# Reloading x for its scaling, and when the weight additions and gate stores of twelve tile pairs are issued, in a hybrid decoder step

## The chip, the cores and the metric

The kernel runs on one core of a Trainium2 chip. The metric is device time in microseconds for one execution of the whole step, lower being better. TensorE (PE) does the matmuls, VectorE (DVE), ScalarE (ACT) and GpSimd (POOL) work on tiles in on-chip memory, and SyncE (SP) issues most transfers. A transfer is issued from an engine's instruction queue, in that queue's order; if it must wait for something, what stands behind it in the queue waits too.

## The reference

One layer: an RMSNorm, one wide input projection that is split into column groups, two branches (sparse attention and an mLSTM recurrence) for a prompt of 1024 tokens and eight decode requests, and one output projection.

```python
h = x * rsqrt(mean(x * x) + eps) * norm_w                # x: 1024 prompt rows + 8 sample rows, 2048 wide
aq, ak, av, iq, ik, iw, az, mq, mk, mv, mi, mf, mo, mz = split(h @ w_in)
att   = sparse_attend(aq, ak, av, top_k(indexer(iq, ik, iw)))        # prompt
att_s = the same for 8 requests, keys and values gathered from a paged cache
h_ml  = mlstm(mq, mk, mv, mi, mf)                        # in chunks of 64, carrying C, n, m
a     = att * silu(az)
mo    = rmsnorm(h_ml) * ml_norm_w * sigmoid(mo) * silu(mz)
y     = final_rmsnorm(x + concat(a, mo) @ w_out)
```

## The kernel before

**Data.** x lies transposed on chip: 16 row groups of 128 model rows, each with R = 1032 columns (1024 prompt tokens and 8 samples). Every f32 operand of a product is split into a high and a low part, and a product is three matmuls (high by high, low by high, high by low). The first 256 columns of x are in tiles named xP, the next 776 in xQ, of which the first four row groups have the last 388 in xR; psum tiles are `pj` and `bank`.

**Tiles.** The input projection runs over 61 tiles of 128 output columns, in the order of `T_MISC` (0), index queries (1 to 8), attention keys `T_AK` (9), values (11), queries (13), mLSTM queries, keys and values (21, 25, 29), gates `T_G` (37 to 52, for each head the output gate and the SiLU gate) and `T_AZ` (53 to 60). A tile is four quarters of four row groups. `proj()` loads a weight quarter (`wraw`, L219), splits it on ACT (L222, wH) and DVE (L223, wL), and multiplies (L1368).

**Start.** Tiles 0 to 2 run on x before it is scaled, since the reciprocal norm `rstd` is not known yet. During tiles 3 to 8 `rescale(k)` turns row group k into x times `rstd` (`norm_w` having been multiplied in at loading): DVE adds high and low (L1456) and multiplies (L1457), ACT makes the new high part (L1458), DVE the low one (L1459), and for k of 8 and up SyncE stores the row to `xS` (L1461). `sums(k)` makes sums and differences of scaled rows k and k + 4 (L1466 to L1469, `y` being 128 x 1032) and stores them to `sS` (L1470, L1471). Which of them follows which quarter stands in `plan` and `slots`. Tiles 4, 5 and 6 multiply unscaled quarters first and scaled ones last.

**Pairs.** From `T_S` (37) on, the tiles go in 12 pairs, in two phases of half of the row groups each: 24 pair-products v, worked in the manner of Strassen with fewer products (P0, P1, A11, A12, A22, S1 to S4) on sums of weights and of x. That is what `sS` is for. In a pair-product (L1591 for its matmuls):
- `wfetch()` loads weights; for two of the sums of weights (T1 in `wraw`, T3 in a slot named xP) SyncE loads one quarter (L1567, L1570) and GpSimd at once issues a second transfer that adds the other to it (L1568, L1571);
- `split()` makes high and low parts (L1576 on ACT, L1577 on DVE);
- `seed()` copies one psum tile to another, on ACT (L1671), for the product that goes on from it;
- `out()` takes results from psum (L1604, L1606, L1608). In phase 1 they are stored to `part`; in phase 2 GpSimd adds `part` to them by an accumulating transfer (L1613, xR<-part; the tiles are eight, in a ring), and the result's `use()` is put on the list `later`;
- `flush(2)` takes uses off that list until two are left. A use of a gate tile is a sigmoid on ACT (L1650, L1653), a product on DVE for the second tile of a pair (L1651), the product of both on GpSimd (L1656) and a store to `gateS` from SyncE (L1657). A use of a `T_AZ` tile multiplies by broadcast row factors (`rb`, loaded into an `ev` buffer; L1662 and L1664 on DVE), takes the sigmoid (L1665), the product on GpSimd (L1666) and stores (L1667).

**Side work.** Attention, index and mLSTM work is cut into pieces, in two lanes, each with jobs that follow one another. `Lane.step()` issues pieces after each quarter (or each `side(now)` of a pair-product) so that a job of a given weight ends at its due tile, the second number of `Job`. A job starts when its start tile is reached, the job before it in its lane is done, and its condition holds: prompt attention `att` waits for decode attention `datt`, `ml` follows `att`.

**Order.** Within these program sections a scheduler puts the instructions of each engine in order at build time, with the sections under `tc.high_priority()` or `hi()` first. After that, each engine executes in order.

## Time and profile before

| | |
|---|---|
| time, median of 2 runs | 2207.28 us (2202.98 to 2211.59) |
| the profiled execution's own time | 2206.24 us |
| its span in the trace | 2204.5 us |
| mean granted TensorE clock | 0.962 |
| busy in the span: PE / DVE / ACT / POOL | 93% / 56% / 46% / 16% |
| bytes moved | 319.58 MB, mean 145 GB/s |

An engine's busy share is an average over the whole span; the page also cuts the span in 40 slices of 55 us, one digit each in tenths. A stretch in which TensorE shows less than 9 is one in which something else ends last, and the lists of waits for that stretch say what: engine and line that waited, the instruction it waited for, then microseconds in total, the number of waits and the longest. A group of instructions is shown as line, engine, operation, tiles, count, busy us, mean ns, and the idle time ahead of them with what ended it.

### The profile page before, as it was taken

How to read it: one execution, taken by the hardware profiler on the slowest of the kernel's cores; microseconds unless marked ns; L12 is line 12 of the kernel's file. 1: busy time of each engine (PE TensorE's matmuls, PEld its weight loads, DVE VectorE, ACT ScalarE, POOL GpSimd, SP SyncE). 2: the span in 40 equal slices, each digit the busy share in tenths (PEclk: the TensorE clock that was granted, in tenths of full speed). 3: DMA queues.
4: the chain of work that ended last, by engine and by line, in shares of the span. 5: the costliest groups of instructions: out<-in, count | busy, mean ns of one | idle time of the engine just before them, and what ended most of it. 6: DMA issues, size and time to landing. Idle time of an engine off the chain costs nothing. (4 is left out here: it accounts for less than half of the span.)

```text
span 2204.5 us, 34897 instructions
## 1 busy us (share of the span) xinstructions
PE 2039.9 (93%) x12390; PEld 1945.4 (88%) x12390; DVE 1242.7 (56%) x2936; ACT 1017.7 (46%) x2114; POOL 342.6 (16%) x390
## 2 busy tenths in 40 slices
PE   9897999999999999869999999887797787999998
PEld 8896999999999999769999999887787777998886
DVE  8794354365554547835666655865665465656331
ACT  8232247733336773124555555654555243433221
POOL 0220111100000000410000001233334451111110
PEclk9998999999999999969999999999899898999999
DMA  6455543322222223626464446877687788648212
GB/s 229 116 179 166 164 130 96 107 85 71 74 68 63 63 65 77 195 78 184 128 164 136 123 106 194 241 202 185 165 230 146 154 246 293 187 152 293 86 62 97
DMA packets 239995, 319.58 MB, mean 145 GB/s; under 512 B 39397, under 2 KB 151973, under 8 KB 239821
## 3 DMA queue, kind: packets, MB, share of 16 engines
q1 hardware_dynamic: 217293, 278.01, 40.6%
q0 software_dynamic: 21376, 37.86, 9.5%
q8 instruction: 97, 1.59, 0.3%
q10 hardware_dynamic: 1152, 1.49, 0.2%
q14 instruction: 77, 0.63, 0.1%
HBM read 238.41 MB, written 78.86 MB: 144 GB/s over the span
## 5 line engine op out<-in xcount | busy, mean ns | idle before, releaser
L1368 PE MATMUL pj<-xQ,wH 128*128 128x388 f32 (+1 forms) x1832 | 484.1, 342 | 20.6 <-ACT xQ L1458 14.8
L1591 PE MATMUL pj<-xQ,wH 128*128 128x388 f32 x1344 | 374.6, 359 | 65.0 <-ACT pj L1671 52.3
L222 ACT CAST wH<-wraw 128x512 fp32r<-128x512 f32 (+2 forms) x279 | 169.6, 611 | 430.3 <-PE pj L1368 194.7
L1368 PEld LDWEIGHTS pj<-xQ,wH 128*128 128x128 f32 (+1 forms) x1832 | 328.9, 189 | 26.1 <-ACT xQ L1458 16.0
L223 DVE TENSOR_TENSOR wL<-wraw,wH 128x512 fp32r<-128x512 f32 (+2 forms) x279 | 193.5, 700 | 237.2 <-ACT wH L222 230.4
L1591 PEld LDWEIGHTS pj<-xQ,wH 128*128 128x128 f32 x1344 | 256.4, 200 | 71.1 <-ACT pj L1671 56.3
L1368 PE MATMUL pj<-xQ,wL 128*128 128x388 f32 (+1 forms) x916 | 312.6, 342 | 0.5 <-DVE wL L223 0.5
L1591 PE MATMUL pj<-xQ,wL 128*128 128x388 f32 x672 | 238.3, 355 | 1.2 <-DVE wL L1577 1.2
L1368 PE MATMUL pj<-xP,wH 128*128 128x256 f32 (+1 forms) x896 | 175.5, 286 | 1.3 <-ACT wH L222 1.1
L1368 PEld LDWEIGHTS pj<-xQ,wL 128*128 128x128 f32 (+1 forms) x916 | 172.9, 189 | 1.6 <-DVE wL L223 0.7
L1577 DVE TENSOR_TENSOR wL<-xP,wH 128x512 fp32r<-128x512 f32 x168 | 118.4, 708 | 61.8 <-ACT wH L1576 57.5
L1591 PE MATMUL pj<-xP,wH 128*128 128x256 f32 x768 | 146.1, 284 | 3.4 <-ACT xP L1543 3.4
L1368 PEld LDWEIGHTS pj<-xP,wH 128*128 128x128 f32 (+1 forms) x896 | 145.1, 188 | 3.9 <-ACT wH L222 1.7
L1576 ACT CAST wH<-xP 128x512 fp32r<-128x512 f32 x168 | 103.0, 615 | 75.1 <-PE pj L1591 63.4
L1591 PEld LDWEIGHTS pj<-xQ,wL 128*128 128x128 f32 x672 | 133.6, 199 | 2.2 <-DVE wL L1577 2.1
L1368 PE MATMUL pj<-xP,wL 128*128 128x256 f32 (+1 forms) x448 | 126.4, 282 | 3.6 <-DVE wL L223 3.6
L1591 PEld LDWEIGHTS pj<-xP,wH 128*128 128x128 f32 x768 | 122.6, 191 | 4.3 <-ACT xP L1543 3.6
L462 ACT ACTIVATE rl<-bank 128x512 f32<-128x512 f32 (+2 forms) x160 | 79.1, 522 | 78.9 <-PE bank L460 53.6
L465 DVE SCALAR_TENSOR_TENSOR s<-rl,wiN,s 128x512 f32<-128x512 f32 (+2 forms) x150 | 94.7, 656 | 35.5 <-ACT rl L462 33.0
L1591 PE MATMUL pj<-xP,wL 128*128 128x256 f32 x384 | 109.0, 284 | 0.9 <-DVE wL L1577 0.9
L1863 PE MATMUL bank<-mH,wH 128*128 128x392 f32 x256 | 89.3, 349 | 16.6 <-ACT wH L222 14.6
L505 ACT ACTIVATE gt<-s,sm 128x384 bf16<-128x384 f32 (+5 forms) x96 | 84.6, 881 | 24.1 <-DVE sm L527 17.7
(457 smaller groups left out, 4372.0 us busy)
## 6 DMA issues: line engine op xcount, KB each, us to landing
wraw<-in_wa_dram SPq DMA_DIRECT2D x166, 256.0 KB
xP<-in_wa_dram SPq DMA_DIRECT2D x120, 256.0 KB
wraw<-in_wo_dram SPq DMA_DIRECT2D x64, 256.0 KB
wraw<-in_wt_dram SPq DMA_DIRECT2D x64, 256.0 KB
part<-ev SPq DMA_DIRECT2D x48, 194.0 KB
xR<-part POOLq DMA_DIRECT2D x48, 194.0 KB
qkv<-mlS SPq DMA_DIRECT2D x16, 512.0 KB
xr<-in_xT_dram SPq DMA_DIRECT2D x14, 516.0 KB
```

What stands on the lines that cost most here:

```text
L222: a = SC.copy(H[:, s, :cols], raw[:, s, :cols])
L223: return a, V.tensor_tensor(L[:, s, :cols], raw[:, s, :cols], H[:, s, :cols].bitcast(F32), OP.subtract)
L462: SC.activation(r[:, :cn], p[:, :cn], AF.Relu)
L465: v = V.scalar_tensor_tensor(s[:, c0:c0 + cn], r[:, :cn], wv, s[:, c0:c0 + cn], OP.mult, OP.add)
L505: SC.activation(junk[:, :W], src[q][:, :W], AF.Sign, bias=bias[:, q:q + 1], scale=scale, accum_out=cnt[:, q:q + 1])
L1368: m = PE.matmul(ps[:cols, :cn], w_[:, k, :cols], xv(kk, xz, c0, cn), start=(n0 == 0 and k == 0 and z == 0), stop=(n0 == n9 and k == 3 and ...
L1576: SC.copy(H, src)
L1577: V.tensor_tensor(L, src, H.bitcast(F32), OP.subtract)
L1591: PE.matmul(ps[:, :n], w_[:, k, :], REG[reg][k](xz), start=(first and k == 0 and z == 0), stop=(last and k == 3 and z == 2), skip_group_ch ...
L1863: PE.matmul(p, w_[:, k, :], x_, start=(n == 0), stop=(n == 47))
```

## The change

Five things are edited.

1. **Scaling.** `xfetch()` loads the rows of x anew, the first five in advance and then one for each row that is scaled. `rescale(k)` multiplies such a row by `norm_w` and `rstd` in one DVE instruction over all 1032 columns (L1459), makes high (L1462) and low parts (L1463) from it, and stores all 16 rows to `xS` (L1464). There is one in each of 16 slots; `sums` is gone from there.
2. **Sums of x.** `xsums()` makes them in tiles 10 to 17: four loads from `xS` into `ev` buffers, the four DVE instructions, four stores to `sS`.
3. **Weight additions.** `wfetch()` only notes them in `adds`; `addup()` issues them (L1587), once after the first part's result and once before the third's.
4. **Gate uses.** The gates' product is on DVE (L1672) in place of GpSimd; the stores to `gateS` are issued by GpSimd (L1673, L1683) in place of SyncE; `flush(3)` leaves three uses on the list.
5. **Due times** of two jobs: prompt attention 47 for 46, decode attention 35.5 for 34.

```diff
@@ -1316,11 +1316,11 @@
 
     lanes = [Lane([Job("gates", T_AK, T_AK + 1.5, 8500, job_gates),
                    Job("index", T_AK, 30.0, 3000 + sum(map(ix_weight, groups)), lambda: job_index(groups)),
-                   Job("att", T_MQ, 46.0, 2 * 2 * sum(2 * (1 + (i + 1) * 0.5) for i in range(8)) + 6, job_att, att_free),
+                   Job("att", T_MQ, 47.0, 2 * 2 * sum(2 * (1 + (i + 1) * 0.5) for i in range(8)) + 6, job_att, att_free),
                    Job("ml", T_G, T_PRE, 38, job_ml)]),
              Lane([Job("dscore", T_AK, 18, 16 + 128 + 2, job_dscore),
                    Job("dsel", T_AK, 30.0, 2000 + 31 * 1700 + 10000 + 16 * 2800 + 2000, job_dsel),
-                   Job("datt", T_MQ, 34.0, 7500 + 8 * 5000 + 4000 + 8 * 2500 + 3000, job_datt, ix_free),
+                   Job("datt", T_MQ, 35.5, 7500 + 8 * 5000 + 4000 + 8 * 2500 + 3000, job_datt, ix_free),
                    Job("dml", T_G, T_PRE - 0.5, 20000 + 16 * 2500 + 5000, job_dml, dml_free)])]
     gateV = gateS.rearrange("(k p) r -> k p r", p=128)
     mixb = [[None] * KT for _ in CB]
@@ -1449,38 +1449,31 @@
                 evac(t, pss[t], 128, iqp)
         ys = {}
 
+        def xfetch(n):
+            for k in range(len(ys), min(KT, n)):
+                y = ys[k] = rp.tile([128, R], F32, name="y")
+                pin(SY.dma_start(y, A["xT"][k]))
+
         def rescale(k):
-            y = ys[k] = rp.tile([128, R], F32, name="y")
+            y = ys[k]
+            V.scalar_tensor_tensor(y, y, nw[:, k:k + 1], rstd, OP.mult, OP.mult)
             for c0, cn in CH if k < 4 else (CH[0], (PN, R - PN)):
-                h, l, e = xv(k, 0, c0, cn), xv(k, 1, c0, cn), y[:, c0:c0 + cn]
-                V.tensor_tensor(e, h.bitcast(F32), l.bitcast(F32), OP.add)
-                V.tensor_tensor(e, e, rstd[:, c0:c0 + cn], OP.mult)
-                SC.copy(h, e)
-                V.tensor_tensor(l, e, h.bitcast(F32), OP.subtract)
-            if k >= K_KEPT:
-                SY.dma_start(xS[k], y)
-
-        def sums(k):
-            y1, y2 = ys[k], ys[k + 4]
-            a11, a21, a12, a22 = (y[:, PN + x * HN:PN + x * HN + HN] for y in (y1, y2) for x in range(2))
-            V.tensor_tensor(a22, a22, a21, OP.subtract)
-            V.tensor_tensor(a21, a11, a21, OP.subtract)
-            V.scalar_tensor_tensor(a11, a22, -1.0, a11, OP.mult, OP.subtract)
-            V.scalar_tensor_tensor(a12, a11, -1.0, a12, OP.mult, OP.subtract)
-            SY.dma_start(sS[k], y1[:, PN:R])
-            SY.dma_start(sS[k + 4], y2[:, PN:R])
-
-        r, z = rescale, sums
-        plan = [(r, 0), (r, 1), (r, 2), (r, 3), (r, 4), (z, 0), (r, 5), (z, 1), (r, 6), (z, 2), (r, 7), (z, 3),
-                (r, 8), (r, 9), (r, 10), (r, 11), (r, 12), (z, 8), (r, 13), (z, 9), (r, 14), (z, 10), (r, 15), (z, 11)]
-        slots = {(3, 0): 1, (3, 1): 1, (3, 2): 1, (3, 3): 1, (4, 0): 1, (4, 1): 1, (4, 2): 1, (4, 3): 1, (5, 0): 2,
-                 (5, 1): 2, (5, 2): 1, (5, 3): 1, (6, 0): 1, (6, 1): 2, (6, 2): 2, (6, 3): 2, (7, 0): 2, (7, 1): 1}
+                h = xv(k, 0, c0, cn)
+                SC.copy(h, y[:, c0:c0 + cn])
+                V.tensor_tensor(xv(k, 1, c0, cn), y[:, c0:c0 + cn], h.bitcast(F32), OP.subtract)
+            SY.dma_start(xS[k], y)
+            xfetch(k + 6)
+
+        plan = list(range(KT))
+        slots = {(3, 0): 1, (3, 1): 1, (3, 2): 1, (3, 3): 1, (4, 0): 1, (4, 1): 1, (4, 2): 1, (4, 3): 1, (5, 1): 1,
+                 (5, 2): 1, (5, 3): 1, (6, 0): 1, (6, 1): 1, (6, 2): 1, (6, 3): 1, (7, 0): 1}
 
         def after(t, n):
             with tc.high_priority():
                 for _ in range(slots.get((t, n), 0)):
-                    f, k = plan.pop(0)
-                    f(k)
+                    rescale(plan.pop(0))
+
+        xfetch(5)
 
 
         for t in range(3, T_AK):
@@ -1503,8 +1496,25 @@
                 evac(t, ps, 128, iqp)
             if t == 3:
                 index_weights(misc)
+    def xsums(t, q):
+        k = t - T_AK - 1
+        if q or not 0 <= k < 8:
+            return
+        k += k // 4 * 4
+        a11, a21, a12, a22 = (evp.tile([128, CN], F32, name="ev") for _ in range(4))
+        for x, (l, r) in enumerate(((a11, a21), (a12, a22))):
+            for y, e in enumerate((l, r)):
+                SY.dma_start(e, xS[k + 4 * x][:, PN + y * HN:PN + y * HN + HN])
+        V.tensor_tensor(a22, a22, a21, OP.subtract)
+        V.tensor_tensor(a21, a11, a21, OP.subtract)
+        V.scalar_tensor_tensor(a11, a22, -1.0, a11, OP.mult, OP.subtract)
+        V.scalar_tensor_tensor(a12, a11, -1.0, a12, OP.mult, OP.subtract)
+        for x, (l, r) in enumerate(((a11, a21), (a12, a22))):
+            for y, e in enumerate((l, r)):
+                SY.dma_start(sS[k + 4 * x][:, y * HN:y * HN + HN], e)
+
     for t in range(T_AK, T_S - 2):
-        pss = proj((t,))
+        pss = proj((t,), after=xsums)
         with tc.high_priority():
             evac(t, pss[0], 128)
 
@@ -1547,6 +1557,7 @@
     slot = [None] * 8
     t1s = {}
     later = []
+    adds = []
     B11, B21, T2, T1, B22, B12, T3, T4 = range(8)
     hi = tc.high_priority
 
@@ -1565,10 +1576,15 @@
         elif j == T1:
             t1s[v] = wst.tile([128, 4, 128], F32, name="wraw", bufs=2)
             SY.dma_start(t1s[v], a1)
-            G.dma_start(t1s[v], b1, accum_op=OP.add)
+            adds.append((t1s[v], b1))
         elif j == T3:
             SY.dma_start(slot[j], b1)
-            G.dma_start(slot[j], b2, accum_op=OP.add)
+            adds.append((slot[j], b2))
+
+    def addup():
+        while adds:
+            t_, w_ = adds.pop(0)
+            G.dma_start(t_, w_, accum_op=OP.add)
 
     def split(j, v):
         H, L = (wst.tile([128, 4, 128], F32R, name="w" + x, bufs=3) for x in "HL")
@@ -1653,8 +1669,8 @@
                 SC.activation(e[:, :cn], e[:, :cn], AF.Sigmoid)
             if (n, c) in keep:
                 o = keep.pop((n, c))
-                G.tensor_tensor(e[:, :cn], o[:, :cn], e[:, :cn], OP.mult)
-                SY.dma_start(gateS[(8 + gi) * 128:(9 + gi) * 128, c0:c0 + cn], e[:, :cn])
+                V.tensor_tensor(e[:, :cn], o[:, :cn], e[:, :cn], OP.mult)
+                G.dma_start(gateS[(8 + gi) * 128:(9 + gi) * 128, c0:c0 + cn], e[:, :cn])
             else:
                 keep[n, c] = e
         else:
@@ -1664,7 +1680,7 @@
                 V.tensor_copy(rb[:, cp:cn], e[:, cp:cn])
             SC.activation(e[:, :cn], e[:, :cn], AF.Sigmoid)
             G.tensor_tensor(e[:, :cn], e[:, :cn], rb[:, :cn], OP.mult)
-            SY.dma_start(gateS[j * 128:(j + 1) * 128, c0:c0 + cn], e[:, :cn])
+            G.dma_start(gateS[j * 128:(j + 1) * 128, c0:c0 + cn], e[:, :cn])
 
     def seed(dst, src):
         if "index" in lanes[0].done:
@@ -1715,8 +1731,10 @@
 
     pj = [psj.tile([128, 512], F32, name=f"pj{c}") for c in range(3)]
     now = T_S * 4
+    addup()
     wfetch(T1, 0)
     wfetch(T1, 1)
+    addup()
     with hi():
         w0 = split(B11, 0)
     product(w0, pj[0], "A11", True, True)
@@ -1748,13 +1766,14 @@
         product(w1, C_, "P1", False, True)
         product(w1, B_, "A12", False, True)
         with hi():
+            addup()
             out(v, 0, 0, C_)
             w1 = split(T1, v)
             if move:
                 f2 = fill_load("A12", nx)
                 fill(f1)
                 fill(f2)
-        flush(2)
+        flush(3)
         side(now)
         product(w2, A_, "S2", False, True)
         with hi():
@@ -1771,10 +1790,11 @@
             w1 = split(B12, v)
             if move:
                 f2 = fill_load("S1", nx)
-        flush(2)
+        flush(3)
         side(now + 1)
         product(w2, B_, "S4", False, True)
         with hi():
+            addup()
             out(v, 1, 1, B_, sv)
             if move:
                 fill(f1)
@@ -1792,7 +1812,7 @@
                 fill(f1)
                 f3 = fill_load("P1", nx)
             w0 = split(B11, v + 1) if v + 1 < len(seq) else None
-        flush(2)
+        flush(3)
         side(now + 2)
         product(w2, A_, "S3", False, True)
         with hi():
@@ -1815,7 +1835,7 @@
                 fill(f2)
         if t >= T_AZ + 3 or pair_tiles(n)[1] == T_G - 1:
             flush()
-        flush(2)
+        flush(3)
         side(now + 3)
         now += 4
     flush()
```

The scheduler's order shows the change at three places. First VectorE, while x is scaled in tiles 4 to 6, before (y is a row of x; L223 splits weights for the tiles; iqe is an evacuation):

```order
L1466 TENSOR_TENSOR y<-y 128x388
L740 SCALAR_TENSOR_TENSOR fx<-fx,t_2058 32x128
L357 TENSOR_TENSOR iqe<-pj_1273,rstd 128x388
L223 TENSOR_TENSOR wL<-wraw,wH 128x512
L1466 TENSOR_TENSOR y<-y 128x388
L1467 TENSOR_TENSOR y<-y 128x388
L742 SCALAR_TENSOR_TENSOR b<-fx 32x128
L1467 TENSOR_TENSOR y<-y 128x388
L1468 SCALAR_TENSOR_TENSOR y<-y 128x388
L749 COPY e_2135<-b 32x1
L223 TENSOR_TENSOR wL<-wraw,wH 128x512
```

and in the changed kernel:

```order
L223 TENSOR_TENSOR wL<-wraw,wH 128x512
L1459 SCALAR_TENSOR_TENSOR y<-y,nw,rstd 128x1032
L742 SCALAR_TENSOR_TENSOR b<-fx 32x128
L1463 TENSOR_TENSOR xP_174<-y,xP_174 128x256
L1463 TENSOR_TENSOR xQ_160<-y,xQ_160 128x776
L223 TENSOR_TENSOR wL<-wraw,wH 128x512
L1459 SCALAR_TENSOR_TENSOR y<-y,nw,rstd 128x1032
L749 COPY e_2055<-b 32x1
L1463 TENSOR_TENSOR xP_175<-y,xP_175 128x256
L1463 TENSOR_TENSOR xQ_161<-y,xQ_161 128x776
L1459 SCALAR_TENSOR_TENSOR y<-y,nw,rstd 128x1032
```

Between two weight splits stood sums of two rows; now the scalings of the next rows stand there, one instruction of 1032 columns and two subtractions each.

Second TensorE, in tiles 33 to 36, where decode attention ends (L1256 to L1289, whose last are matmuls of four columns on gathered values) and prompt attention begins (L574, L611). Before:

```order
L1256 MATMUL bank<-cst,lT 64x128
L1258 MATMUL bank<-onesf,kn 64x1
L1256 MATMUL bank<-cst,lT 64x128
L1276 MATMUL bank<-cst,P 128x64 x2
L1277 MATMUL bank<-cst,pb 128x64
L1289 MATMUL bank<-PT,kv 128x4 x32
L574 MATMUL bank<-cst,pP 128x128 x8
L611 MATMUL bank<-kH,qH 128x512
L611 MATMUL bank<-kL,qH 128x512
```

and now, from the same place on:

```order
L1276 MATMUL bank<-cst,P 128x64 x2
L1277 MATMUL bank<-cst,pb 128x64
L1289 MATMUL bank<-PT,kv 128x4 x12
L1368 MATMUL bank<-xP_175,wH 128x256 x2
L1368 MATMUL bank<-xP_175,wL 128x256
L1368 MATMUL bank<-xP_175,wH 128x256 x2
L1368 MATMUL bank<-xP_175,wL 128x256
L1368 MATMUL bank<-xP_175,wH 128x256 x2
L1368 MATMUL bank<-xP_175,wL 128x256
L1368 MATMUL bank<-xP_175,wH 128x256 x2
L1289 MATMUL bank<-PT,kv 128x4
L1368 MATMUL bank<-xP_175,wL 128x256
```

The L1289 matmuls were all together with L574 right behind them; now products of the projection (L1368) stand between them, and L574 comes some fifty rows later.

Third GpSimd in phase 2, in pair-products of the gate tiles (L841, L840, L872 to L874 are mLSTM side work). Before:

```order
L1613 DMA xR_10543<-part_9718 128x256
L1568 DMA wraw<-in_wa_dram 128x512
L1613 DMA xR_10544<-part_9718 128x388
L841 TENSOR_SCALAR aL<-onec 128x2x2
L1571 DMA xP_10104<-in_wa_dram 128x512
L1613 DMA xR_10544<-part_9718 128x388
L840 CAST aH<-onec 128x2x2
L1613 DMA xR_10545<-part_9718 128x256
L1656 TENSOR_TENSOR xR_10544<-xR_10544 128x388
L1613 DMA xR_10545<-part_9718 128x388
```

and now:

```order
L1629 DMA xR_10304<-part_9565 128x388
L1587 DMA xP_9844<-in_wa_dram 128x512
L1673 DMA gateS<-xR_10303 128x388
L1629 DMA xR_10301<-part_9565 128x256
L841 TENSOR_SCALAR aL<-onec 128x2x2
L840 CAST aH<-onec 128x2x2
L1629 DMA xR_10301<-part_9565 128x388
L1673 DMA gateS<-xR_10304 128x388
L872 TENSOR_SCALAR st<-st 128x2
L873 TENSOR_TENSOR st<-st,mhalf 128x2
L1673 DMA gateS<-xR_10301 128x256
```

The weight additions (L1568, L1571, now L1587) stood between accumulations of results; the products (L1656) are gone from this queue, and stores to `gateS` (L1673) have come, each behind some later accumulations.

## The prediction

> **What bounds the kernel now.** I read the page first, for the engine that the time belongs to, then the same engine in stretches of the span, and then only what it waits for in the stretches where it is short. Parts 1 and 2 of the page:
>
> ```profile
> PE 2039.9 (93%) x12390; PEld 1945.4 (88%) x12390; DVE 1242.7 (56%) x2936; ACT 1017.7 (46%) x2114; POOL 342.6 (16%) x390
> PE   9897999999999999869999999887797787999998
> PEclk9998999999999999969999999999899898999999
> ```
>
> TensorE is the bound, and most of its slices are full. It is short in four places: near the start, at the 19th and 20th slice, in the long run from the 26th on, and once near the end. Nothing outside them can bring time, because the change takes no matmul away. The table of windows gives their size (columns: window, length, PE busy and its matmuls, granted clock, DMA share, GB/s; two rows also have the busy times of PEld, DVE, ACT and POOL, in this order):
>
> ```profile
> 60.00:200.00 140.00, 116.36 (x615) 0.90 0.56 168
> 100.00:110.00 10.00, 10.00 (x58) 1.00 0.76 216
> 300.00:500.00 200.00, 200.00 (x1343) 198.91 (x1342) 97.46 (x258) 117.13 (x280) 23.32 (x28) 1.00 0.32 97
> 850.00:900.00 50.00, 50.00 (x352) 1.00 0.53 152
> 900.00:1000.00 100.00, 72.78 (x386) 0.78 0.39 115
> 1250.00:1300.00 50.00, 50.00 (x336) 1.00 0.34 93
> 1404.00:1773.00 369.00, 294.26 (x1739) 283.11 (x1739) 212.31 (x620) 184.83 (x392) 133.41 (x185) 0.91 0.76 186
> ```
>
> I turn counts into lost time. **A**, 60 to 200 us (tiles 3 to 8, x being scaled): a full 10 us holds 58 matmuls, so 615 need 106 us and 34 are lost. **B**, 900 to 1000 (tiles 33 to 35, decode attention ending and prompt attention beginning): at 352 in 50 us, 386 need 55 and 45 are lost, though some of them are tiny. **C**, 1404 to 1773, ten pair-products of the second phase: at 336 in 50 us, 1739 need 259 and 110 are lost, 11 in each of 36.9. **D** is the switch to the output projection near 1840.
>
> **A: scaling.** The waits of PE and DVE, then the groups of DVE, in 60 to 200 us:
>
> ```profile
> PE pj L1368 <- ACT xQ L1458: 14.8, 2, 9.4
> PE pj L1368 <- ACT xR L1458: 4.5, 1, 4.5
> DVE y L1456 <- DMA sS<-y: 9.4, 6, 4.1
> L1457 DVE TENSOR_TENSOR y<-y,rstd 128x256 f32<-128x256 f32 (+2 forms) x36 | 21.2, 626 | 0.0
> L1459 DVE TENSOR_TENSOR xQ<-y,xQ 128x776 fp32r<-128x776 f32 (+1 forms) x16 | 13.6, 856 | 4.5 <-ACT xQ L1458 4.5
> L1456 DVE TENSOR_TENSOR y<-xQ 128x776 f32<-128x776 f32 (+1 forms) x16 | 13.4, 857 | 0.0
> L1456 DVE TENSOR_TENSOR y<-xP 128x256 f32<-128x256 f32 x16 | 6.4, 420 | 9.5 <-DMA sS<-y 9.4
> L1466 DVE TENSOR_TENSOR y<-y 128x388 f32<-128x388 f32 x8 | 4.4, 554 | 0.9 <-DMA xS<-y 0.9
> ```
>
> PE waits for ACT's copies, ACT's copies wait for DVE: VectorE is the bound here. The change takes away the additions of high and low part (13.4 + 6.4), the multiplications (21.2), and the sums (four lines with the same eight operations, 4 x 4.4 = 17.6): 58.8 us. It adds 16 fused multiplications of 128x1032. No row has that width; 857 ns for 776 columns makes 1.14 us, so 16 x 1.14 = 18 us. VectorE does 40 us less in a stretch of 140. What remains on DVE behind ACT is L1459 (now L1463).
>
> Against it stands the load. Sixteen rows of 516 KB come in anew (8.3 MB), all 16 rows are stored instead of 8 (4.1 MB more), and the sums' stores go (16 x 388 KB, 6.2 MB): 6.2 MB more on 140 us x 168 GB/s = 23.5 MB. At the same rate per busy share, 0.56 becomes 0.71. The window at 100 us shows 0.76 beside 58 matmuls, so this share alone doesn't hold PE up. But in SyncE's order the row loads stand behind the stores of tile 3 and the fifth weight load, and the first scaling can't begin before they land. Bounds: all 34 us come back, or the rows land late and 5 us are lost, which is a 516 KB load at 150 GB/s (3.4 us) with the half clock after it. I take 16, about half: the freed VectorE time covers the loss fully, but tiles 4 and 5 will wait for data at their start.
>
> The sums come back in tiles 10 to 17, in a stretch that the row of 300 to 500 us shows: PE full, DVE at 49%, DMA share 0.32. The cost there is 8 x 4 x 0.554 = 18 us of DVE and 12.4 MB of loads and stores; over eight tiles (about 170 us at 144 matmuls each and the row's pace) that is 73 GB/s beside 97, and the share goes from 0.32 to some 0.56. PE was still full at 0.53 in the row of 850 us, and at 0.76 in that of 100 us. Bounds 0 and 18 (all of DVE's work in the way); I take **3**, near the hidden end, for the evacuation buffers that the sums share with the tiles.
>
> **B: side work's due times.** In 900 to 1000 us PE waits for these, and spends 14.7 us on 64 matmuls of four columns:
>
> ```profile
> PE bank L574 <- DMA pP<-avS: 7.7, 1, 7.7
> PE bank L653 <- ACT pP L627: 4.3, 2, 3.2
> PE bank L1276 <- DVE P L1270: 2.5, 1, 2.5
> PE bank L1289 <- DMA kv<-in_cv_dram,idxs: 2.4, 4, 0.6
> PE bank L1256 <- DVE lT L1248: 2.4, 1, 2.4
> ```
>
> None is long; they hurt since no product stands between them. The new due times make the decode attention end 1.5 tiles later. In the changed order products follow the first of the L1289 matmuls, and some fifty rows of products stand ahead of L574. That covers the 7.7 us and the gather's waits; the waits on DVE (L1256, L1276) stay as they were. The loss lies between the waits shown (19.3) and the count (45), so some 33; I take half, **17**, with bounds 0 (the wait moves to the next side job) and 45.
>
> **C: phase 2.** One stall, from the timelines of POOL, ACT and PE:
>
> ```profile
> 1459.76 0.88 POOL L1571 DMA_DIRECT2D xP<-in_wa_dram  x1 [9.79 <-DMA xP<-in_wa_dram]
> 1460.31 3.04 POOL L1613 DMA_DIRECT2D xR<-part  x3
> 1467.91 0.53 ACT L1650 ACTIVATE ev<-xR 128x388 f32<-128x388 f32 x1 [6.30 <-DMA xR<-part]
> 1473.59 0.47 ACT L1671 COPY pj<-pj 128x388 f32<-128x388 f32 x1
> 1474.11 1.02 PE L1591 MATMUL pj<-xQ,wH 128*128 128x388 f32 x2 [5.39 <-ACT pj L1671]
> ```
>
> POOL stands behind a weight load for 9.8 us; three accumulating transfers come out only then; ACT stands at a sigmoid for the first of them; the seed behind it on ACT is late; and PE waits 5.4 us, then starts slowly: 1.02 us for two matmuls, where the full window above holds one in 0.15. Over 1400 to 1800 us the sums are:
>
> ```profile
> PE pj L1591 <- ACT pj L1671: 50.2, 14, 6.2
> PE pj L1591 <- DVE xR L1604: 10.5, 4, 4.2
> ACT ev L1650 <- DMA xR<-part: 66.8, 19, 8.4
> ACT xR L1653 <- DMA xR<-part: 36.7, 17, 4.6
> POOL xP L1571 <- DMA xP<-in_wa_dram: 59.2, 9, 9.8
> SPq L1657 <- POOL xR L1656: 60.1, 17, 10.1
> POOL xR L1666 <- ACT xR L1665: 42.4, 9, 7.5
> L1613 POOL DMA_DIRECT2D xR<-part x67 | 63.8, 998 | 61.4 <-DVE xR L1606 23.8 <-ACT xR L1608 19.1 <-DVE xR L1604 9.1
> L1656 POOL TENSOR_TENSOR xR<-xR,xR 128x256 f32<-128x256 f32 (+1 forms) x16 | 15.4, 962 | 16.2 <-ACT xR L1653 9.8 <-DMA gateS<-xR 5.2 <-DVE xR L1651 0.8
> ```
>
> Three edits meet this chain. The weight additions, issued later, take POOL's waits (59.2 / 9 = 6.6 us each) from in front of the accumulations. flush(3) puts one more evacuation between an accumulation and its sigmoid; there are six in a pair-product, so 36.9 / 6 = 6.2 us more, against mean waits of 66.8 / 19 = 3.5 and 36.7 / 17 = 2.2. The stores, off SyncE, free it of 60.1 us of standing, in which loads and other stores queue. So ACT's 103.5 us of waits should mostly go. What they are worth on PE: its two waits are 60.7 us in 18 pieces; the granted clock of 0.91 over 369 us is 33 us of clock lost, 1.8 or some 2 for each restart; 97 in all, near the 110 of the count. By the window's row ACT is idle for half the time (184 of 369, so some 200 of 400 us), of which the accumulations end 103.5, 52%; I credit the same share of the stalls, 50 us. From this go 5 us because prompt attention ends a tile later and the mLSTM work has one pair-product less, and 3 because POOL gets more work: 40 of the 48 stores at some 1.0 us (the price of L1613's issue) for the 24 gate multiplications at 0.96, so 40 - 23 = 17 us more beside its idle 236. C: **42**, with bounds 0 and 97. The multiplications go to DVE at the 388-column price of L1466, 24 x 0.55 = 13 us. I put nothing on them: DVE is busy 212 of 369 us, and its idle time hides them; uncovered, ahead of the evacuations of L1604, they cost 13.
>
> On the stores the Trainium skill ("DMA: Bandwidth & Descriptors", section "Issuing engines are not separate DMA queues") says that transfers of all issuing engines share the same 16 DMA engines, and that issuing elsewhere saves only the sequencer's time. The row SPq L1657 shows something else to be saved, a wait of 3.5 us each; by the page's rule the edit would be worth nothing on PE, which is part of rival 1 below.
>
> **D: the switch.** PE waits 14.6 us for the first output weights' split, which stands behind the last gate stores:
>
> ```profile
> PE bank L1863 <- ACT wH L222: 14.6, 1, 14.6
> ```
>
> Stores off SyncE let those weight loads go earlier; but the tail still is sigmoid, multiplication, store, reload of the gated rows, and the store now costs an issue on POOL. Bounds -6 and +6; I take **+1**.
>
> **Sum.** 16 + 17 + 42 - 3 - 1 = 71. The profiled execution took 2206.2 us, 1 below the median: 2206 - 71 = **2135**.
>
> **Rivals.** *1: C stays.* The transfer's own latency sets ACT (the stall above shows 1460.3 to 1467.9, 7.6 us from the first issue to the sigmoid), POOL's stores replace POOL's waits, and the ACT queue finds other things to stand behind, such as rows that wait for DVE. Then A and B bring 33, less 4: 2177. For it: the three accumulations came out together, so their landing is slow by itself; DMA share is 0.76. Against it: flush(3) gives more than the mean wait. *2: all of it comes,* 34 + 45 + 97 less 4: 2034; with half of the rest that I left, about 2085. Against it: the stretches also have waits that nothing in the change touches (L1604 10.5, L1256, L1276). *3: slower, by POOL's queue.* POOL executes in order. Each of 48 stores waits there for a multiplication, which waits for a sigmoid, which waits for an accumulation; later accumulations and weight additions stand behind it, where before SyncE did the waiting. If each store holds POOL as long as L1657 held SyncE (3.5 us), 48 x 3.5 = 168 us of standing come in place of 59 us; with half of it reaching PE, C loses 84 instead of gaining: 2206 - 33 + 4 + 84 = 2261. It breaks even with A and B at 29 / 48 = 0.6 us of each store reaching PE. Against it: in the changed order two or three accumulations stand between one and its store, so most stores find their product ready, and before, L1656 stood in the same queue for the same sigmoid.
>
> **How the numbers follow.** Forecast 0.60, rival 1 0.24, rival 2 0.08, rival 3 0.08. The likeliest case spans 2097 to 2173, by half of C or all of B. Within 2% (the least that a measurement of this kernel tells from no change) means above 2163, and a little of the forecast's case lies there: faster 0.63, same 0.29, slower 0.08. The range takes in rival 1 with some of A or B missing and part of rival 2, and leaves out the ends: 2070 to 2210.
>
> **What would show it.** A: PE's waits for L1458's successor under 8 us, 60 to 200 us with over 700 matmuls; wrong if PE or ACT waits for y's loads. B: no wait of L574 over 2 us. C: pair-products of some 32 us, POOL's wait for xP near zero, ACT's waits on xR<-part below 50 us; wrong if POOL stands at its stores, or if ACT's waits stay while POOL's are gone. D: the wait of L1863 near 14. The sums: no wait of PE in 250 to 500 us.

## The result, and the profile after

The changed kernel takes 2124.97 us (median of 2 runs, 2123.0 to 2126.95) against 2207.28: ratio 0.963, 95% interval 0.954 to 0.972. The profiled execution took 2126.95 us. It is faster by 82 us; 71 were forecast. The page's parts 1 and 2:

```profile
PE 2023.6 (95%) x12390; PEld 1929.7 (91%) x12390; DVE 1220.9 (57%) x2904; ACT 1019.8 (48%) x2118; POOL 326.7 (15%) x414
PE   9999999999999999989999999998889778999998
PEclk9999999999999999979999999999999898999999
```

The early dent is gone, the one in the middle is a slice or so, and the long one is still there but shallower. The windows that answer to those of before (PE alone: busy, matmuls, granted clock, DMA share, GB/s):

```profile
60.00:200.00 140.00, 132.24 (x742) 0.98 0.72 229
100.00:150.00 50.00, 45.78 (x243) 0.97 0.98 347
350.00:400.00 50.00, 49.98 (x335) 1.00 0.58 175
900.00:1000.00 100.00, 89.28 (x511) 0.88 0.62 168
1359.00:1743.00 384.00, 335.75 (x2063) 0.95 0.85 211
```

742 matmuls stand in 60 to 200 us where 615 stood, and 511 in 900 to 1000 where 386 stood. Pair-products 12 to 23, the last row, take 384 us; in the kernel before they took 425 (1395 to 1820).

Windows at fixed times slide against the program. So I took marks in the program from the timelines of PE: the start of the 1000th matmul of L1368 (within tile 8), of pair-product 0 (v0), of pair-product 12 (v12, where phase 2 begins; a pair-product is 132 matmuls of L1591, now L1607, so this is the 1585th of them), the last pair-product's end, and the last matmul of the output projection. For each the time is given against the kernel before, in its profiled execution:

| us against before | tile 8 | v0 | v12 | last product | end |
|---|---|---|---|---|---|
| changed kernel | -18.3 | -54.0 | -36.4 | -77.0 | -80.0 |

So A brought 18. The sums in tiles 10 to 17 took next to nothing (the difference is -18.0 at the 4650th matmul of L1368, ahead of decode attention's end). B brought 36 up to v0, of which 18 are given back between v0 and v12. C brought 41, and D 3. A mark is one execution: this kernel and the eight of the second table below run the same program as far as tile 8, and their marks there differ by 3 us.

### The profile page after: what moved, and what is told of

It is laid out like the page before. It is cut to its first block, busy times and chain, and to the rows that moved or that the text cites. A ratio compares the mean times of both kernels' runs of the same rounds, so it can differ in the third digit from the quotient of the medians.

```text
span 2125.1 us, 34960 instructions
## 1 busy us (share of the span) xinstructions
PE 2023.6 (95%) x12390; PEld 1929.7 (91%) x12390; DVE 1220.9 (57%) x2904; ACT 1019.8 (48%) x2118; POOL 326.7 (15%) x414
## 3 DMA queue, kind: packets, MB, share of 16 engines
q0 software_dynamic: 24192, 46.32, 11.1%
## 4 chain that ended last, share of the span: by engine, by line
PE 69%; DMA 15%; DVE 6%; issue 4%; ACT 3%; POOL 1%; SPq 1%; DVEq 0%; POOLq 0%; ACTq 0%
PE pj L1368 27%; PE pj L1607 11%; PE bank L1883 6%; PE bank L1921 6%; PE pj L1921 4%; DMA xR<-part 4%; PE bank L460 3%; PE bank L662 2%; PE bank L1368 2%; DMA xP<-in_wa_dram 2%; PE bank L611 2%; PE bank L653 1%; PE bank L973 1%; DMA qkv<-mlS 1%; DMA y<-in_xT_dram 1%
## 5 line engine op out<-in xcount | busy, mean ns | idle before, releaser
L1368 PE MATMUL pj<-xQ,wH 128*128 128x388 f32 (+1 forms) x1832 | 479.8, 340 | 3.5 <-ACT wH L222 1.7
L1607 PE MATMUL pj<-xQ,wH 128*128 128x388 f32 x1344 | 366.1, 351 | 31.9 <-ACT pj L1687 22.5
L1368 PEld LDWEIGHTS pj<-xQ,wH 128*128 128x128 f32 (+1 forms) x1832 | 327.1, 188 | 6.9 <-ACT wH L222 2.4
L223 DVE TENSOR_TENSOR wL<-wraw,wH 128x512 fp32r<-128x512 f32 (+2 forms) x279 | 193.6, 701 | 241.2 <-ACT wH L222 228.6
L1368 PE MATMUL pj<-xQ,wL 128*128 128x388 f32 (+1 forms) x916 | 310.5, 340 | 0.7 <-DVE wL L223 0.6
L1607 PEld LDWEIGHTS pj<-xQ,wH 128*128 128x128 f32 x1344 | 248.0, 194 | 38.5 <-ACT pj L1687 26.1
L1607 PE MATMUL pj<-xQ,wL 128*128 128x388 f32 x672 | 233.7, 349 | 0.6 <-DVE wL L1593 0.5
L1368 PE MATMUL pj<-xP,wH 128*128 128x256 f32 (+1 forms) x896 | 175.6, 286 | 2.1 <-ACT wH L222 1.1
L1368 PEld LDWEIGHTS pj<-xQ,wL 128*128 128x128 f32 (+1 forms) x916 | 171.6, 187 | 2.2 <-DVE wL L223 1.3
L1607 PE MATMUL pj<-xP,wH 128*128 128x256 f32 x768 | 149.0, 287 | 3.5 <-ACT xP L1553 1.4
L1368 PEld LDWEIGHTS pj<-xP,wH 128*128 128x128 f32 (+1 forms) x896 | 145.5, 189 | 4.7 <-ACT wH L222 1.8
L1593 DVE TENSOR_TENSOR wL<-xP,wH 128x512 fp32r<-128x512 f32 x168 | 119.8, 716 | 51.9 <-ACT wH L1592 50.2
L1607 PEld LDWEIGHTS pj<-xQ,wL 128*128 128x128 f32 x672 | 130.0, 193 | 1.6 <-DVE wL L1593 1.3
L1368 PE MATMUL pj<-xP,wL 128*128 128x256 f32 (+1 forms) x448 | 127.0, 284 | 4.3 <-DVE wL L223 4.3
L1607 PEld LDWEIGHTS pj<-xP,wH 128*128 128x128 f32 x768 | 123.6, 192 | 5.9 <-ACT xP L1553 1.7
L1607 PE MATMUL pj<-xP,wL 128*128 128x256 f32 x384 | 109.9, 286 | 5.6 <-DVE wL L1593 5.6
```

Source lines behind the costliest of these rows:

```text
L223: return a, V.tensor_tensor(L[:, s, :cols], raw[:, s, :cols], H[:, s, :cols].bitcast(F32), OP.subtract)
L1368: m = PE.matmul(ps[:cols, :cn], w_[:, k, :cols], xv(kk, xz, c0, cn), start=(n0 == 0 and k == 0 and z == 0), stop=(n0 == n9 and k == 3 and ...
L1593: V.tensor_tensor(L, src, H.bitcast(F32), OP.subtract)
L1607: PE.matmul(ps[:, :n], w_[:, k, :], REG[reg][k](xz), start=(first and k == 0 and z == 0), stop=(last and k == 3 and z == 2), skip_group_ch ...
```

## The experiments

Marks are against the kernel before for the first four runs, against the changed kernel for the others; times are medians, ratios are to the kernel before on the same chip. The changed kernel itself has only two times, so its own ratio is the widest (0.954 to 0.972).

### Each part alone

**Scaling alone**: the kernel before, with `xfetch`, the new `rescale` and `slots`, and `xsums`.

> The kernel before with the new scaling and the moved sums alone. By the theory of three separate places it gains what the change gained ahead of tile 9, 18 us, all of it before 220 us of the span, and nothing later: 2189. The rival, that an earlier start of the later tiles meets the same stalls in attention and phase 2 at other times and loses it there, expects 2200 to 2207.

**Due times alone:**

```diff
-                   Job("att", T_MQ, 46.0, ...
+                   Job("att", T_MQ, 47.0, ...
-                   Job("datt", T_MQ, 34.0, ...
+                   Job("datt", T_MQ, 35.5, ...
```

> The kernel before with the two due times (47, 35.5) alone. The theory: tiles 33 to 36 gain 38 us as in the changed kernel, since products stand among decode attention's small matmuls, and the first phase of the pairs gives some 18 back, since prompt attention has moved into it: 2187. Rival 1: the 18 us in the first phase come from the other edits (weight additions issued late), then 2169. Rival 2: without the relieved engines of the other edits the products find nothing to cover, 2200 to 2207.

**Phase 2's edits alone**: the kernel before, with `adds` and `addup`, the gate product on DVE, the stores from GpSimd, and `flush(3)`.

> The kernel before with the late weight additions, the gate product on VectorE, the stores from GpSimd and three uses kept, nothing else. Theory: phase 2 gains 41 us as in the changed kernel, phase 1 nothing: 2166. Rival: a part of those 41 is the attention work that the due times took out of phase 2 or put there; then 2175 to 2190. If phase 1 loses the 18 us here, the late additions are their cause, and the time is some 2184.

**The sums moved, without the reload:** the scaling by addition and multiplication, `xsums` as changed, all 16 rows stored.

```diff
-            if k >= K_KEPT:
-                SY.dma_start(xS[k], y)
+            SY.dma_start(xS[k], y)
...
-    (sums(k) and its slots)
+    (xsums in tiles 10 to 17, one rescale in each of 16 slots)
```

> The kernel before with the sums of x moved to tiles 10 to 17 and all 16 rows stored, but the rows still put together on chip from high and low part (no reload). It takes 17.6 us of VectorE's work out of the scaling, where the change takes 40. Theory (VectorE's time is what counts): 17.6 / 40 of 18 us, so 8 gained, 2199. Rival: the sums' stores, for which the row buffers wait, were what held it; then all 18, 2189. Second rival: the reload alone matters, then 2207.

| run | us | ratio (95%) | tile 8 | v0 | v12 | last product | end |
|---|---|---|---|---|---|---|---|
| scaling alone | 2188.4 | 0.993 (0.990 to 0.995) | -21.4 | -18.1 | -16.7 | -21.3 | -19.9 |
| due times alone | 2173.7 | 0.986 (0.983 to 0.990) | +1.9 | -38.7 | -17.8 | -35.1 | -34.8 |
| phase 2's edits alone | 2191.9 | 0.993 (0.991 to 0.996) | -0.1 | +1.2 | +4.8 | -11.1 | -12.4 |
| sums moved, no reload | 2193.3 | 0.994 (0.992 to 0.996) | -14.3 | -11.5 | -9.7 | -15.5 | -14.2 |

Scaling keeps its 18 to 20 to the end. The due times alone make all of B's gain at v0 and give 21 back by v12, but gain 17 more in phase 2 where I had booked a loss. Phase 2's edits alone bring 16 there (from +4.8 to -11.1), not 41. The parts sum to 19 + 34 + 15 = 68 us, 14 short of the change.

With the sums moved and no reload, two thirds of A are there at tile 8 (14.3 of 21.4). Its waits of PE from 60 to 215 us, and its window:

```profile
PE pj L1368 <- ACT xR L1458: 4.5, 1, 4.5
PE pj L1368 <- ACT wH L222: 3.9, 2, 3.3
60.00:200.00 140.00, 126.99 (x703) 0.96 0.55 166
```

The two waits on L1458's xQ (14.8 us) are gone with the sums alone, which are 17.6 of the 58.8 us of DVE's work: they stood between one row's scaling and the next. The time, 2193, lies between the 2199 that VectorE's work would give and the 2189 of the rival, by which the sums' stores held the row buffers. DVE's 9.4 us of waits for those stores are gone here too, so this run doesn't tell the work from the stores.

### The changed kernel with one edit undone or taken further

**The due times of before:**

> The changed kernel with the due times of before (46 and 34). The parts alone gave 19 (scaling), 34 (due times) and 15 (phase 2's edits), 68 together, and the change gave 82. If the missing 14 lie between the due times and phase 2's edits, both wanted for the same stalls in pair-products 12 to 23, this takes 2125 + 34 + 14 = 2173 and phase 2 gains little over before. If the parts add up and the 14 are elsewhere (scaling with phase 2's edits), 2159.

**Two uses kept:**

```diff
-        flush(3)
+        flush(2)
```

> The changed kernel with flush(2) in place of flush(3). Theory of the prediction: the one more evacuation between an accumulation and its sigmoid is what takes ACT's waits, so pair-products 12 to 23 lose some 20 us: 2145. Rival (the late additions alone free the accumulations): 2125 to 2130. Second rival (fewer kept results free the ring of eight and the buffers of the last pairs): a few us faster, 2120.

**Weight additions at once:**

```diff
-            adds.append((t1s[v], b1))
+            G.dma_start(t1s[v], b1, accum_op=OP.add)
...
-            adds.append((slot[j], b2))
+            G.dma_start(slot[j], b2, accum_op=OP.add)
```

> The changed kernel with the weight additions issued right behind their loads, as before. Theory of the prediction: GpSimd stands some 6 us at each third sum of weights, and the accumulations behind it come late: 10 to 20 us lost in pair-products 12 to 23, none in the first phase, where nothing is accumulated: 2135 to 2145. Rival (with three results kept, the accumulations have time enough): 2125 to 2128.

**Gate stores from SyncE** (both `G.dma_start(gateS...` are `SY.dma_start(gateS...`):

> The changed kernel with the gate stores issued by SyncE again (the product stays on VectorE). Theory of the prediction: SyncE stands some 60 us at them and weight loads queue behind: 10 us lost, 2135. Rival (the issuing engine saves only its issue time): 2125. Second rival (GpSimd's queue, freed of stores, lets accumulations go earlier): 2115 to 2120.

**Only prompt attention due at 46 again:**

> The changed kernel with prompt attention due at 46 again, decode attention still at 35.5. Undoing both cost 50 us: 38 at tiles 33 to 36, 18 of it given back in the first phase, and 18 more in pair-products 12 to 23. Theory: the 38 are decode attention's due time alone; those 18 in phase 2 are prompt attention's, since mLSTM's work (which follows it) then begins later, out of the change of phases: 2125 + 18 less the few us that the first phase gets back, 2138 to 2143. Rival: phase 2's gain is no matter of where mLSTM's work lies but of decode attention's shift too: 2125 to 2130.

**Prompt attention due at 48:**

> The changed kernel with prompt attention due at 48 in place of 47. If a later start of mLSTM's work is what helped phase 2, a smaller step of the same sign: 2110 to 2120. If mLSTM, squeezed into one pair-product less, is what then ends last, 2130 to 2140.

**Four uses kept** (`flush(4)`):

> The changed kernel with four uses kept (flush(4)). Going from three to two cost 21 us. ACT still waits 73 us for accumulations in phase 2: if the distance to the sigmoid is still what counts, another 5 to 15 us go, 2110 to 2120. Rival: the ring of eight result tiles and the five ev buffers of the last pairs run short, 2130 to 2140.

**The gate product on GpSimd again:**

```diff
-                V.tensor_tensor(e[:, :cn], o[:, :cn], e[:, :cn], OP.mult)
+                G.tensor_tensor(e[:, :cn], o[:, :cn], e[:, :cn], OP.mult)
```

> The changed kernel with the gate product on GpSimd again (stores stay on GpSimd's queue). The prediction put the product's move at nothing, GpSimd having time: 2125. Rival: GpSimd's queue, which now also issues the stores, stands longer at each product, and accumulations behind it come late: 2130 to 2140.

| run (marks against the changed kernel) | us | ratio to before (95%) | v0 | v12 | last product | end |
|---|---|---|---|---|---|---|
| due times 46 and 34 | 2176.6 | 0.987 (0.984 to 0.990) | +38.2 | +22.8 | +40.7 | +42.5 |
| prompt attention 46 | 2155.9 | 0.978 (0.976 to 0.980) | -1.4 | +1.8 | +30.3 | +31.5 |
| prompt attention 48 | 2137.2 | 0.969 (0.967 to 0.971) | -0.5 | -8.4 | +13.3 | +14.5 |
| flush(2) | 2146.6 | 0.972 (0.969 to 0.975) | -1.7 | +1.6 | +18.0 | +21.2 |
| flush(4) | 2138.0 | 0.969 (0.968 to 0.971) | +2.0 | +4.7 | +14.7 | +14.8 |
| additions at once | 2128.7 | 0.965 (0.963 to 0.968) | -2.5 | +0.6 | +0.2 | +0.7 |
| stores from SyncE | 2141.9 | 0.970 (0.967 to 0.973) | -0.7 | -0.7 | +17.8 | +17.7 |
| product on GpSimd | 2135.7 | 0.969 (0.967 to 0.971) | -4.0 | -2.5 | +7.8 | +8.1 |

**B is decode attention's due time alone**: with prompt attention back at 46, v0 begins where it does in the changed kernel (-1.4). **The late additions are worth nothing** that can be measured. **Stores, uses kept and product** cost 18, 21 and 8 us of span when undone, nearly all of it behind v12, which is where they act. **The due times and the other edits need each other**: without the new due times the time is 2177, as expected (2173) if the missing 14 us lie between the two. (The profiled execution of that run is its fastest, 7 us below the median.)

What frees GpSimd from its weight waits is seen in its waits in pair-products 12 to 23, first with the additions at once, then with the stores from SyncE (and SyncE's largest at these stores), each with the other edits in place:

```profile
POOL xP L1582 <- DMA xP<-in_wa_dram: 28.7, 8, 7.0
```

```profile
POOL xP L1587 <- DMA xP<-in_wa_dram: 52.5, 8, 10.8
SPq L1673 <- DVE xR L1672: 10.8, 5, 4.2
SPq L1683 <- POOL xR L1682: 10.9, 5, 5.8
```

The changed kernel has 28.2 in 9 (below). Issued late or at once, an addition to xP waits some 3.3 us for its first load; with the stores on SyncE it is 6.6 us, just as before (59.2 in 9). Over all its waits at the two lines, SyncE stands 47.5 us at 45 stores there (30.8 at L1673, 16.7 at L1683). The stores are not the only thing that sets these waits: with flush(2), stores on GpSimd, they are 39.9 in 8.

How this reaches PE is another chain than the prediction's, for PE's wait for the seeds isn't longer with the stores on SyncE (19.7 us, against 21.6). The longest stall of that run, from the timelines of POOL, DVE and PE:

```profile
1655.21 0.90 POOL L1587 DMA_DIRECT2D xP<-in_wa_dram  x1 [5.64 <-DMA xP<-in_wa_dram]
1656.83 0.88 POOL L1629 DMA_DIRECT2D xR<-part  x1
1667.68 0.56 DVE L1678 TENSOR_TENSOR ev<-ev,xR 128x388 f32<-128x388 f32 x1 [10.96 <-DMA xR<-part]
1670.24 0.86 DVE L878 TENSOR_SCALAR hm<-bank,st 128x256 f32<-128x256 f32 x2
1670.77 0.47 PE L886 MATMUL bank<-cst,hm 128*128 128x128 f32 x1 [9.58 <-DVE hm L878]
```

GpSimd waits for a weight load, the accumulation behind it goes out that much later and is read 10.9 us after its issue, DVE stands at the use of a `T_AZ` tile for it, and behind that in DVE's queue is a step of the mLSTM (L878) on which PE waits. PE waits 18.8 us for L878 in that run, 4.6 in the changed kernel. How much of it the 5.6 us of GpSimd's wait make, and how much the accumulation's own time, isn't told apart; the DMA engines were full meanwhile (share 1.01 from 1657 to 1668 us).

With flush(2), ACT's and PE's waits in the same pair-products, and one stall in the timelines of ACT and PE:

```profile
ACT ev L1666 <- DMA xR<-part: 53.9, 19, 7.7
ACT xR L1669 <- DMA xR<-part: 35.7, 20, 4.7
PE bank L852 <- ACT dH L796: 18.6, 5, 6.0
1460.33 0.53 ACT L1666 ACTIVATE ev<-xR 128x388 f32<-128x388 f32 x1 [7.70 <-DMA xR<-part]
1460.76 0.39 ACT L796 CAST dH<-d 128x256 fp32r<-128x256 f32 x1
1461.30 0.55 PE L852 MATMUL bank<-aH,dH 128*128 128x258 f32 x1 [5.96 <-ACT dH L796]
```

ACT waits 90 us for accumulations, against 73 with three kept. PE shows its loss at an mLSTM matmul (L852), whose split stands right behind such a sigmoid on ACT: 18.6 us here, 2.1 in the changed kernel.

With four kept, ACT's waits for accumulations fall only to 68 us, and the kernel is slower. GpSimd stands at the stores longer (1360 to 1760 us):

```profile
POOL gateS L1673 <- DVE xR L1672: 36.9, 10, 7.3
```

and with the product on GpSimd it stands at that (same window):

```profile
POOL xR L1672 <- DVE xR L1667: 54.1, 17, 9.3
```

That these two reach PE is likely, but no chain to PE was followed.

**Why do due times matter in phase 2?** They act in two pair-products, and in every kernel. Pair-product 12, where phases change and x's parts are exchanged, takes 33.6 to 42.6 us in the six kernels with prompt attention due at 46 and 25.1 to 30.7 in the eight with 47 or 48. Pair-product 20, the first with a `T_AZ` tile, takes 39.5 to 43.2 us in the six and 27.1 to 33.5 in the eight. These two hold the 31 us that due at 46 costs beside the other edits: 18 in pair-product 12 (42.6 against 25.1) and 13 in pair-product 20 (42.1 against 28.6). I had expected 13 to 18 in all.

In pair-product 12 of the run at 46 PE has 60 matmuls of side work where the changed kernel has 34, and sits idle for 10.6 us, against 0.4. One wait there, 1325 to 1400 us:

```profile
PE pj L1607 <- ACT wH L1592: 5.7, 1, 5.7
```

That is the theory, at the right spot: mLSTM work that follows prompt attention meets the exchange. In pair-product 20 of the same run a chain leads to a late seed (timelines of POOL, DVE, ACT and PE, then the window):

```profile
1653.69 0.87 POOL L1629 DMA_DIRECT2D xR<-part  x1 [1.09 <-ACT xR L1624]
1664.51 0.43 DVE L1678 TENSOR_TENSOR ev<-ev,xR 128x256 f32<-128x256 f32 x1 [7.24 <-DMA xR<-part]
1664.97 0.42 ACT L1681 ACTIVATE xR<-xR 128x256 f32<-128x256 f32 x1 [8.75 <-DVE ev L1678]
1668.14 1.01 PE L1607 MATMUL pj<-xQ,wH 128*128 128x388 f32 x2 [7.04 <-ACT pj L1687]
1653.00:1664.00 11.00, 7.96 (x48) 1.00 0.98 131
```

and the same place in the changed kernel:

```profile
1629.21 0.92 POOL L1629 DMA_DIRECT2D xR<-part  x1 [0.15 <-issue]
1632.33 0.42 DVE L1678 TENSOR_TENSOR ev<-ev,xR 128x256 f32<-128x256 f32 x1 [0.58 <-DMA xR<-part]
1629.00:1633.00 4.00, 4.00 (x28) 1.00 0.59 106
```

The accumulation that the first `T_AZ` use needs is read 10.8 us after its issue with prompt attention at 46, and 3.1 us after it in the changed kernel; in all six kernels with 46 it is 9.6 to 12.3 us, in the eight others 3.1 to 5.5. In all six, and in none of the eight, SyncE issues a block of the mLSTM's output (L889) and the final states of its first two heads (L916) within 4 us behind that accumulation. In the run at 46 the DMA engines are full there (share 0.98, against 0.59 in the changed kernel). In seven of the eight the states come 10 us or more behind it; in the eighth, the due times alone, one of the two comes 0.8 us behind, and the 5.3 us to the use are among the longest of the eight. So the due time decides whether the end of the mLSTM's work falls on an accumulation that DVE, and behind it ACT, stands for. That these stores slow it is an inference from fourteen kernels; no run moved them alone.

Due at 48 isn't better: 8 us are gained by v12, and 22 lost after it, where mLSTM's work has fewer pair-products left; I found no single wait for those.

## Why the prediction was right, point by point

2135 was forecast, and 2125 came. A, B and D were right in kind and near in size. C's size was right by luck: of its 41 us, less than half came from the edits that were credited.

**A: right.** 16 forecast, 18 measured. PE's and DVE's waits in 60 to 215 us, then the new instruction:

```profile
PE pj L1368 <- ACT iqe L355: 1.8, 1, 1.8
PE pj L1368 <- ACT wH L222: 1.7, 2, 1.2
DVE y L1459 <- DMA y<-in_xT_dram: 6.7, 5, 3.3
DVE wL L223 <- ACT wH L222: 37.2, 13, 5.8
L1459 DVE SCALAR_TENSOR_TENSOR y<-y,nw,rstd 128x1032 f32<-128x1032 f32 x16 | 20.5, 1284 | 6.7 <-DMA y<-in_xT_dram 6.7
```

PE no longer waits for scaled rows at all, and DVE now waits for ACT. The fused instruction took 1284 ns, where I had 1.14 us: the 857 ns that I scaled was a mean over two shapes ("+1 forms"), twelve of 776 columns at 959 ns and four of 388 at 548, and 959 scaled to 1032 columns is 1.28 us. The rows' loads came late for 6.7 us, as feared. At 58 matmuls per 10 us, 742 need 128 of the 140 us, so 12 are still lost of A's 34, 8 of them from 100 to 150 us, where 243 matmuls stand and the DMA engines were at 0.98 (window above), far above the 0.71 that I had spread evenly over the stretch. That the full DMA engines cost these 8 is not shown: with the sums moved and no reload the same window holds 220 matmuls at a share of 0.60.

**The sums: right in sign, small.** Share 0.58 where 0.56 was forecast, PE full; 0.3 us here and one or two in the kernels that share this part, against 3.

**B: right, 17 forecast and 18 net.** PE's waits in 850 to 1000 us, and the cover in the timeline:

```profile
PE bank L1276 <- DVE P L1270: 2.5, 1, 2.5
PE bank L1256 <- DVE lT L1248: 2.4, 1, 2.4
PE bank L574 <- DMA pP<-avS: 1.8, 2, 1.5
937.04 0.42 PE L1289 MATMUL bank<-PT,kv 128*128 128x4 f32 x2
937.32 0.67 PE L1368 MATMUL bank<-xQ,wH 128*128 128x388 f32 x1
937.79 0.93 PE L1289 MATMUL bank<-PT,kv 128*128 128x4 f32 x6
```

L574's 7.7 us became 1.8, and the two waits on DVE stayed as said. Products fill prompt attention's first waits too. Half of the 36 us at v0 is no gain but work put off, which I hadn't listed: 156 of prompt attention's 1024 matmuls (L574, L611, L653, L662) stood ahead of v0 before, and 26 do now. The other 130 are some 18 us at the row's pace of 352 in 50 us, and 18 come back in the first phase.

**C: the size right (42, measured 41) by luck, its parts wrong.** In the changed kernel, pair-products 12 to 23:

```profile
PE pj L1607 <- ACT pj L1687: 21.6, 11, 4.3
ACT ev L1666 <- DMA xR<-part: 39.6, 15, 5.3
ACT xR L1669 <- DMA xR<-part: 33.1, 14, 4.7
ACT xR L1681 <- DVE ev L1678: 39.9, 12, 8.6
POOL xP L1587 <- DMA xP<-in_wa_dram: 28.2, 9, 6.5
POOL gateS L1673 <- DVE xR L1672: 23.8, 9, 7.6
```

The seeds' wait went from 50.2 to 21.6, the chain that the prediction followed. But of its three edits the first, the late additions, does nothing; GpSimd's wait for xP halved with the stores off SyncE, and didn't go to "near zero". ACT's 103.5 us went to 73 only, so "should mostly go" was too much, and the threshold for ACT (below 50) was missed. Yet the time came, and a pair-product takes the 32 us that were named (384 / 12). ACT's longest wait is now for rows that DVE makes (L1681, 39.9 us in 12; before, L1665, 45.5 in 13), which the prediction had left to rival 1.

What failed is the credit of 50 us for these edits: they bring 16 alone, and 18 beside the new scaling (419.6 us for pair-products 12 to 23 against 401.5). And I subtracted 5 us for prompt attention ending later, where the due times in fact gave 17 alone and 18 with the other edits. The new scaling alone gives 5 more there. So the sum came out right with two errors that cancelled.

On the stores, the Trainium skill ("DMA: Bandwidth & Descriptors", section "Issuing engines are not separate DMA queues") would have had the issuing engine matter for the sequencer's time only. Here it mattered by 17 us. That doesn't contradict the sharing of the DMA engines: what was saved, as far as the waits tell, is place in an in-order queue ahead of weight loads.

**Rival 1** (C stays) was nearer to what phase 2's edits did alone, 16 us, than the 50 that I credited. **Rival 3** (GpSimd stands at the stores) is real and small: 23.8 us in the 9 waits shown and 31 in all, at 44 stores, so 0.7 us each where it supposed 3.5; 24 of the 44 show no wait, for the reason given.

**D: a little better than forecast:** 3 us gained against 1 lost; the wait for the first output weights:

```profile
PE bank L1883 <- ACT wH L222: 12.6, 1, 12.6
```

**Where the parts don't add up.** Taking the three parts' marks together, pair-product by pair-product, they give the changed kernel's within 1.6 us up to pair-product 11, and, after up to 13 us of difference in pair-products 12 to 16, within 3.2 again at the starts of pair-products 17 to 20. Then 12 us part them in pair-product 20 alone: it takes 39.5 us before, 43.2 with the scaling, 42.6 with phase 2's edits and 33.5 with the due times, and 28.6 with all. In all six kernels with prompt attention due at 46 the seed's stall shown above is there (5.5 to 7.7 us), and in none of the eight others is it over 3.2.

**What stays open.** Each of five neighbours of the changed kernel (attention a tile earlier or later, one use less or more kept, the product on GpSimd) is 8 to 31 us slower, in phase 2. For attention a tile earlier, flush(2) and the stores the waits show a chain. For attention a tile later, four uses kept and the product I can't separate a mechanism from a scheduled order that happens to fit: every edit moves all that follows it in the queues. That would take kernels with a fixed order, which were not tried.

## What to carry to other kernels

Where an engine's queue executes in order, a store that waits for its data is a wait for all behind it: put it on a queue where what stands behind is not urgent, and test that by itself. Side work that waits on transfers is cheap when products stand between its pieces and dear when pieces stand together; the due time of the job that ends decides that, and also what its last transfers collide with. When a gain at one place is work put off, look where it comes back. And when a change has several edits, run each alone and each undone: here one did nothing, and one that was booked as a cost of 5 us (prompt attention a tile later) costs 31 when it is undone.

## What the runs showed of the hardware

The stores moved from SyncE's queue to GpSimd's cost the DMA engines nothing more. Queue, packets, MB and share of 16 engines in pair-products 12 to 23, with the stores from SyncE and the rest as changed (402 us):

```profile
q1 hardware_dynamic: 47438, 63.14, 53.6%
q0 software_dynamic: 13172, 17.90, 29.0%
```

and in the changed kernel (384 us):

```profile
q1 hardware_dynamic: 40997, 55.26, 48.2%
q0 software_dynamic: 15729, 25.52, 36.8%
```

GpSimd's queue, q0, rose from 0.290 x 402 = 117 us of all engines to 0.368 x 384 = 141, 25 us for 7.6 MB; SyncE's, q1, fell from 215.5 to 185, 30.5 us for 7.9 MB. That is 3.2 us per MB on the one and 3.9 on the other, and the sums of both queues, 332 and 326 us, are near each other. What is dear on q0 are the accumulations, all that it holds with the stores on SyncE: 117 / 17.9 = 6.5 us per MB, against 3.4 on q1.

A full share doesn't tell the bytes: at 0.98 the DMA engines moved 347 GB/s from 100 to 150 us of the changed kernel, and 131 GB/s in the 11 us of pair-product 20 above, where GpSimd's queue holds two thirds of their time and one accumulation of results, one of weights and one store were issued on it. The highest share of before that I had shown was 0.76.
